# RMSNorm with ReLU on one core: two small zero writes to the output rows, queued between the prefetch loads

## Chip, cores, metric

One core of a Trainium2 chip. Times are device microseconds; a kernel's time is the median of several executions. The span is the profiled part of one execution, about 1.7 us shorter. All runs with a known state were in the fast state, with a granted clock of 1.00; a single run of a kernel has no known state, and its time is only a rough one.

## The reference

```python
# x: (16, 1024, 512) float32, gamma: 512, eps: 1e-5
rms = np.sqrt(np.mean(x ** 2, axis=-1, keepdims=True) + eps)
return np.maximum(x / rms * gamma, 0).astype(np.float32)
```

The 16384 rows of 512 floats are read once and written once: 33.55 MB each way.

## The kernel before

The rows are cut into 8 chunks of 4 MB. In a chunk every one of the 128 partitions holds 16 rows, 32 KB that lie together in HBM. There are six slots in SBUF (the core's on-chip memory), so six chunks are loaded ahead; chunk 0 comes in two halves, so that the computation starts early (ScalarE's first square at 8.78 us). All loads and stores are issued by SyncE (SP) on one queue:

```python
xv = x2.rearrange("(c p k) d -> c p k d", p=P, k=K)      # K = 16
ov = out2.rearrange("(c p k) d -> c p k d", p=P, k=K)
loads = [(0, 0, G), (0, G, K - G)] + [(i, 0, K) for i in range(1, nchunks)]   # G = 8
...
for m, (i, a, r) in enumerate(loads):
    if i < nslots:                      # nslots = 6
        load(m)
nxt = nslots
for i in range(nchunks):
    nc.sync.wait_ge(done, per * (i + 1))      # DVE has finished chunk i
    store(i)
    if i >= 1 and nxt < nchunks:
        nc.sync.wait_ge(sem_st[nxt - nslots], 16)   # the slot is stored
        ...load of chunk nxt...
        nxt += 1
```

ScalarE (ACT) squares and sums the rows and takes the root; VectorE (DVE) takes the reciprocal, multiplies by it and by gamma in place, and applies the maximum in place, in groups of 8 rows per partition.

## Time and profile before

| | before |
|---|---|
| time, median of 6 runs | 162.82 us (162.61 to 162.89) |
| profiled span | 161.2 us |
| DMA bytes | 67.1 MB, 97.4% of 16 engines' span |
| DVE busy / ACT busy | 126.0 / 86.3 us |

The page's groups of instructions (line, engine, operation, tiles, count; busy us, mean ns; idle before them) show where DVE's time goes, and its list of DMA issues (count, KB each, us from issue to landing) how long the transfers lie in the queue:

```profile
L139 DVE SCALAR_TENSOR_TENSOR slots<-slots,rstd,gamma_sb 128x512 f32 x128 | 86.2, 747 | 4.8 <-DVEq L136 4.8
L146 DVE TENSOR_SCALAR slots<-slots x16 | 36.7, 2294 | 2.4 <-DVEq L145 0.2
...
out_dram<-slots SPq DMA_DIRECT2D x8, 4096.0 KB, 31.4
slots<-in_x_dram SPq DMA_DIRECT2D x7, 4096.0 KB, 30.4
```

A 4 MB transfer takes 9.7 us on the engines but 30 us from issue to landing: by these medians some three transfers are queued at a time. DVE works steadily, but its sum is 35 us below the span.

**How the hole is measured.** The trace records every DMA packet. A row of 32 KB takes 1.213 us on its engine. "Hole" below is the extra time over 1.213 us of the last three rows before a change of direction, each row's mean over the 16 engines, summed. The expectations on record used the interval between completions instead, which reads about 0.02 to 0.05 us more.

### The profile page before, as it was taken

The page shows a single profiled execution, that of the slowest core. Times are in us where ns is not written, and L with a number is a line of the kernel's source. Part 1 is how long each engine was busy: PE and PEld are TensorE (multiplying, and loading weights), DVE is VectorE, ACT ScalarE, POOL GpSimd, SP SyncE. Part 2 cuts the span into 40 slices and gives each one's busy share as a digit, 9 for nine tenths or more (in the row PEclk, how much of TensorE's full clock was granted, in tenths as well). Part 3 has the DMA queues.
Part 4 walks back from the last instruction along what each step waited for, and adds up shares of the span by engine and source line. Part 5 has one row for each costly group of instructions (what it writes and reads, how often), then busy time and mean ns, then how long its engine had stood idle before and what let it go on. Part 6 is the DMA issues. An engine that isn't in the chain of part 4 may idle for free. (4 is left out here: it accounts for less than half of the span.)

```text
span 161.2 us, 1006 instructions
## 1 busy us (share of the span) xinstructions
DVE 126.0 (78%) x164; ACT 86.3 (54%) x273; POOL 0.2 (0%) x4
## 2 busy tenths in 40 slices
DVE  1103989898989898999999999999999999993000
ACT  3088929889988988988900298503994000000000
POOL 0000000000000000000000000000000000000000
DMA  5999999999999999999999999999999999999993
GB/s 155 433 439 431 496 390 415 496 390 399 512 390 390 512 399 390 390 399 512 390 399 504 399 399 496 407 399 488 407 407 488 407 407 480 415 407 464 431 390 138
DMA packets 2456, 67.12 MB, mean 416 GB/s; under 512 B 276, under 2 KB 276, under 8 KB 280
## 3 DMA queue, kind: packets, MB, share of 16 engines
q1 hardware_dynamic: 2448, 67.11, 97.4%
q10 hardware_dynamic: 8, 0.01, 0.0%
HBM read 33.56 MB, written 33.55 MB: 416 GB/s over the span
## 5 line engine op out<-in xcount | busy, mean ns | idle before, releaser
L115 ACT ACTIVATE junk<-slots 128x512 f32 x128 | 74.5, 582 | 30.8 <-ACTq L111 30.5
L139 DVE SCALAR_TENSOR_TENSOR slots<-slots,rstd,gamma_sb 128x512 f32 x128 | 86.2, 747 | 4.8 <-DVEq L136 4.8
L146 DVE TENSOR_SCALAR slots<-slots x16 | 36.7, 2294 | 2.4 <-DVEq L145 0.2
L115 ACT ACTIVATION_READ_ACCUMULATOR junk<-slots x128 | 23.9, 187 | 0.0
L133 DVE RECIPROCAL rstd<-rms x16 | 3.2, 197 | 6.4 <-DVEq L129 6.4
L122 ACT ACTIVATE rms<-ss,eps_sb x16 | 4.8, 301 | 3.0 <-ACTq L121 3.0
L126 DVE LOAD_MASK_SELECT gamma_sb<-gseed x1 | 0.0, 14 | 5.8 <-DMA gseed<-in_gamma_dram 5.8
L107 ACT ACT_TABLE_LOAD x1 | 1.3, 1283 | 2.8 <-issue 2.8
L100 DVE MEMSET gseed<- 128x512 f32 x1 | 0.5, 485 | 1.1 <-SPq L81 1.1
L126 DVE STREAM_SHUFFLE gamma_sb<-gseed 128x512 f32<-128x512 f32 x1 | 0.7, 716 | 0.0
L168 POOL MEMSET const-bfloat16-1.0<- 128x1 bf16 x1 | 0.1, 102 | 0.0
L168 POOL MEMSET const-uint8-127<- 128x1 uint8 x1 | 0.1, 102 | 0.0
L168 POOL MEMSET const-float32-1.0<- 128x1 f32 x1 | 0.1, 99 | 0.0
L168 POOL MEMSET const-float32-0.0<- 128x1 f32 x1 | 0.1, 98 | 0.2 <-issue 0.2
L101 DVE MEMSET eps_sb<- 128x1 f32 x1 | 0.1, 59 | 0.0
## 6 DMA issues: line engine op xcount, KB each, us to landing
out_dram<-slots SPq DMA_DIRECT2D x8, 4096.0 KB, 31.4
slots<-in_x_dram SPq DMA_DIRECT2D x7, 4096.0 KB, 30.4
slots<-in_x_dram SPq DMA_DIRECT2D x2, 2048.0 KB, 9.7
gseed<-in_gamma_dram ACTq DMA_DIRECT2D x1, 8.0 KB
```

Source lines behind the costliest of these rows:

```text
L100: nc.vector.memset(gseed, 0.0).then_inc(sem_z, 1)
L101: nc.vector.memset(eps_sb, eps).then_inc(sem_e, 1)
L107: nc.scalar.preload_act_table(ACTF.Sqrt)
L115: a = nc.scalar.activation(out=junk[:, j, :], in_=slots[:, bass.ds(base + j * d, d)], func=ACTF.Square, accum_out=ss[:, bass.ds(col + j, 1)])
L122: nc.scalar.activation(out=rms[:, bass.ds(col, G)], in_=ss[:, bass.ds(col, G)], func=ACTF.Sqrt, bias=eps_sb, scale=inv_d).then_inc(sq, 1)
L126: nc.vector.stream_shuffle(gamma_sb, gseed, [0] * 32)
L133: nc.vector.reciprocal(out=rstd[:, bass.ds(col, G)], in_=rms[:, bass.ds(col, G)]).then_inc(sv, 1)
L139: r = nc.vector.scalar_tensor_tensor(out=row, in0=row, scalar=rstd[:, bass.ds(col + j, 1)], in1=gamma_sb, op0=ALU.mult, op1=ALU.mult)
L146: nc.vector.tensor_scalar_max(out=blk, in0=blk, scalar1=0.0).then_inc(done, 1)
L168: nc = _bacc.Bacc("TRN2", target_bir_lowering=False, num_devices=1)
```

## The change

The intent: the stream loses about 0.7 us where it turns from loads to the first store. Two tiny stores to the rows that the first store will write, called touches below and queued earlier, are to take that cost at a point where it can be hidden. What they write is overwritten by the real store; the changed kernel issues that store only when they have landed (52.37 us).

```diff
+    zeros = singles.tile([P, 32], F32, name="zeros")
+    sem_w = tc.alloc_semaphore("touch")
+    sem_wz = tc.alloc_semaphore("touchz")
...
+        ntouch = 0
         for m, (i, a, r) in enumerate(loads):
             if i < nslots:
                 load(m)
+                if nslots - 3 <= i < nslots - 1 and a + r == K:
+                    if ntouch == 0:
+                        nc.sync.wait_ge(sem_wz, 1)
+                    nc.sync.dma_start(out=ov[0][:, ntouch, 0:32],
+                                      in_=zeros).then_inc(sem_w, 16)
+                    ntouch += 1
+        nc.sync.wait_ge(sem_w, 16 * ntouch)
...
+        nc.vector.memset(zeros, 0.0).then_inc(sem_wz, 1)
```

## The prediction

> **What bounds the kernel now.** I read the page first, then the stages of the span, the landings of each transfer, the waits of the queue that issues the transfers, and the timeline of the end.
>
> The page's busy table, the DMA rows of its slices and its table of queues (packets, MB, share of 16 engines):
>
> ```profile
> DVE 126.0 (78%) x164; ACT 86.3 (54%) x273; POOL 0.2 (0%) x4
> DMA  5999999999999999999999999999999999999993
> q1 hardware_dynamic: 2448, 67.11, 97.4%
> ```
>
> The DMA engines are full from the first microseconds to the end, at 97.4% of 16 engines' span; DVE is busy for 78% of it. The single queue q1 carries all loads and all stores. The packet records of the trace say how it runs: a 32 KB row takes 1.21 us on one of the 16 engines, each engine has 8 of the 128 rows of a transfer, so a 4 MB transfer takes 8 x 1.21 = 9.68 us, and in 16 of the 17 transfers (the two 2 MB ones count as half) one follows the other with no gap. 16 x 9.68 = 154.9 us of the 161.2 us span is therefore bytes. What is left, about 6.3 us, is: 1.95 us until the first packet (0.94 us to the first issue and 1.0 us from there), about 0.8 us in which the first packets are slow, about 1.2 us by which the last DMA engine ends after the first one, 1.6 us after the last data, and one hole in the middle of about 0.7 us.
>
> That hole is what the change is about. In equal stretches of the span, one transfer long (start:end, length, DVE, ACT and POOL busy, clock, DMA share, GB/s):
>
> ```profile
> 41.14:50.82 9.68, 9.23 (x14) 9.21 (x32) 0.00 (x0) 1.00 1.01 433
> 50.82:60.50 9.68, 9.23 (x13) 8.73 (x29) 0.00 (x0) 1.00 1.08 433
> 60.50:70.18 9.68, 9.09 (x13) 8.73 (x29) 0.00 (x0) 1.00 0.91 393
> 70.18:79.86 9.68, 9.23 (x11) 9.21 (x32) 0.00 (x0) 1.00 1.00 430
> 79.86:89.54 9.68, 8.94 (x13) 0.88 (x3) 0.00 (x0) 1.00 1.00 433
> ```
>
> 433 GB/s everywhere, but 393 GB/s in the stretch in which the last prefetched load ends and the first store begins. 40/433 of 9.68 us is 0.9 us, cut by the edges of the stretch; the packet records give the better size. The sixth whole load (chunk 5) has its last two rows on every engine at 1.21 to 1.66 and 1.54 to 1.96 us in place of 1.21, and the first engine's completion comes 10.36 us after that of the load before, not 9.68. So 0.68 us are lost once, at 58.5 to 61.5 us. The later changes from a load to a store and back cost nothing measurable (intervals of 9.68 us again). It is a thing of the first write to the output, or of the first read of SBUF by DMA.
>
> The issuing queue's waits (who, for whom, us in total, times, longest):
>
> ```profile
> SPq L78 <- DVE slots L146: 105.4, 6, 26.6
> SPq L74 <- DMA out_dram<-slots: 32.9, 2, 24.1
> ```
>
> and its timeline in the middle (start, length, what):
>
> ```profile
> 31.14 16.83 SPq L78 DMA_DIRECT2D out_dram<-slots  x2
> 72.07 0.34 SPq L74 DMA_DIRECT2D slots<-in_x_dram  x1
> ```
>
> The queue waits long, but early: the first store is issued at 31.1 and the second at about 48.0, while the engines reach the first store only at 61.5, behind six chunks of loads. The end of the computation against the end of the queue:
>
> ```profile
> 144.20 2.29 DVE L146 TENSOR_SCALAR slots<-slots  x1
> 146.52 0.33 SPq L78 DMA_DIRECT2D out_dram<-slots  x1
> ```
>
> DVE ends at 146.5 and the last store is issued there; the engines finish the store before it at 148.7. With 1.0 us from issue to first packet, the last store is ready about 1.1 us before it is needed. DVE is thus the next bound, close behind.
>
> [...] the store issued at 31.1 moves no byte before 61.5. [...] the 4 B semaphore writes of the trace take 9 ns each and the gamma packets of 2048 B 84 ns. [...] a packet follows a semaphore write within 6 ns.
>
> **The change part by part.**
> 1. DVE: one memset of 128x32, ahead of the one of 128x512. The 128x1 memset took 59 ns and the 128x512 one 485, so about 0.08 us. It delays gamma, which is there at 7.4 us and needed at 15.0: 0.
> 2. Issue: two more transfers at about 0.4 us each on the queue that issues loads, the first behind the fourth chunk's load. The engines have about 40 us of work queued then: 0.
> 3. The new wait before the first store ends when the second small write has landed, behind the fifth chunk. That load ends at about 51.7 us in the trace; [...] the first store is issued at about 54 in place of 31.1, the second directly after it. The engines need it at 61.5. Slack about 7 us: 0. The refill of a slot, issued when the first store has landed (72.1), does not move.
> 4. DMA work: per engine 2 x 8 packets of 128 B and two semaphore writes. If one costs what a 4 B semaphore write costs (9 ns), that is 16 x 9 = 0.15 us; if it costs a gamma packet's 84 ns, 1.3 us. I choose 30 ns: about +0.5 us, all on the path, since the engines have no gap in which to hide it.
> 5. The intended gain: the first-write stall is taken by 128 B writes, [...] and not by a stream of 32 KB writes. At best -0.68 us.
> Sum, if the stall is hidden: 162.7 - 0.7 + 0.5 = 162.5. At the very best 162.0 to 162.1.
>
> **Rivals.**
> A. The stall moves and does not vanish: the ring stops for the first small write as it stopped for the first store. For it: the stall showed in the packets of the load *ahead* of the store, so it may block whatever is in the engine, whatever the size of the write. Against it: nothing. Then 162.7 + 0.5 = 163.2, with a hole at about 42 us instead of 60.
> B. Each small write makes a hole of its own: [...] The start shows what that costs: the first row of 16 KB takes 1.2 to 1.5 us against 0.61, some 0.7 us. Twice that, with or without the stall saved: 163.4 to 164.6. Against it: semaphore descriptors between loads make no hole. [...]
> C. DVE takes over as the bound: it would eat a gain above about 1.1 us. A gain of 0.7 stays below it.
> D. The stall is not tied to writing the output, or is tied to each 4 MB area or row: the touches cover 256 B of each row of chunk 0 alone. Then the stall stays at 60 us and the touches cost 0.5: 163.2. Against the area: the stores of later chunks, to areas never touched, have no stall.
>
> **Range and chances.** Stall hidden (0.45): 162.0 to 162.8. Moved or kept (0.3): 162.9 to 163.6. Own holes (0.2): 163.4 to 164.6. Worse (0.05). The middle of this lies at about 162.7, and I predict 162.6 us, 161.9 to 164.1. Faster by 2% means under 159.5, a gain of 3.2 us, and no term reaches that: 0.01. Slower by 2% means over 165.9, [...]: 0.04. Within 2%: 0.95.
>
> **What would show it.** Right: the stretch at 60 us at about 433 GB/s, packets of 128 B at some tens of ns, no wait at the first store that ends after 61.5, the first store landed at about 71.9 or earlier. Wrong in step 5: a hole near 42 or 52 us of about 0.7, or the one at 60 still there. Wrong in step 4: two slow spots behind the fourth and fifth loads with sum over 1 us. Wrong in step 3: the first store issued after 61.5, with an idle DMA there. Wrong altogether: a last store that waits for DVE, or a time below 161.9.

## The result, and the profile after

| | before | after |
|---|---|---|
| median | 162.82 us (162.61 to 162.89, 6 runs) | 162.88 us (162.74 to 163.09, 6 runs) |
| ratio after/before | | 1.0006 (95%: 0.9993 to 1.0019) |

Ratios here are the mean time of one kernel's fast runs over that of the other's from the same rounds, so not quite the ratio of the medians. Two later comparisons of the same pair on other chips gave 1.0007 (0.9990 to 1.0024) and 1.0000 (0.9987 to 1.0013). The kernels are equal to about 0.2%.

The page after, the rows that answer to those of before (busy, DMA by slices, packets, queue), and the issues of the new transfer:

```profile
DVE 126.1 (78%) x165; ACT 86.3 (54%) x273; POOL 0.2 (0%) x4
DMA  5999999999999999999999999999999999999993
DMA packets 2744, 67.15 MB, mean 417 GB/s; under 512 B 564, under 2 KB 564, under 8 KB 568
q1 hardware_dynamic: 2736, 67.14, 97.6%
...
out_dram<-zeros SPq DMA_DIRECT2D x2, 16.0 KB, 43.4
```

There are 288 packets more: 256 of 128 B and 32 semaphore writes. The other rows of the page differ only in what follows from these, in line numbers and in small scatter. The same equal stretches of the span as for before:

```profile
41.14:50.82 9.68, 9.23 (x14) 9.21 (x32) 0.00 (x0) 1.00 1.02 435
50.82:60.50 9.68, 9.23 (x13) 8.73 (x29) 0.00 (x0) 1.00 1.06 435
60.50:70.18 9.68, 9.08 (x13) 8.73 (x29) 0.00 (x0) 1.00 0.94 406
70.18:79.86 9.68, 9.23 (x11) 9.21 (x32) 0.00 (x0) 1.00 1.00 433
```

The stretches with the touches (41 and 51 us) lose nothing visible. The stretch at 60 us is still the slow one, at 406 GB/s against 393 before: the hole is still there. By packets it is 0.39 us, against 0.72. The GB/s of a stretch only show where the hole lies; for its size they are too coarse, since the hole's place against the stretch's edges counts too. The same stretch of c1_after and of e1_wait_only, two runs told of below:

```profile
60.50:70.18 9.68, 9.08 (x13) 8.73 (x29) 0.00 (x0) 1.00 0.91 393
60.50:70.18 9.68, 9.08 (x13) 8.73 (x29) 0.00 (x0) 1.00 0.92 396
```

The first has a hole of 0.57 us by packets and the second one of 0.78, in the opposite order. So sizes below are by packets.

The issuing queue's waits (who, for whom, us in total, times, longest), and its timeline (start, length, what):

```profile
SPq L77 <- DMA out_dram<-slots: 27.2, 2, 18.8
SPq L100 <- DVE slots L160: 25.5, 1, 25.5
SPq L81 <- DMA out_dram<-zeros: 21.2, 1, 21.2
```

```profile
3.63 0.47 SPq L94 DMA_DIRECT2D out_dram<-zeros  x1
4.14 0.44 SPq L77 DMA_DIRECT2D slots<-in_x_dram  x1
4.63 0.49 SPq L94 DMA_DIRECT2D out_dram<-zeros  x1
...
52.38 0.82 SPq L81 DMA_DIRECT2D out_dram<-slots  x2
71.98 0.34 SPq L77 DMA_DIRECT2D slots<-in_x_dram  x1
```

The new wait of 21.2 us looks large in a list of waits and costs nothing: it ends at 52.4 us, and the engines reach the first store at 61.4. The refill of the first slot is issued at 71.98 us, against 72.07 before.

How small the cost of a touch is, the DMA summary of the 1.5 us around the first of them shows:

```profile
DMA packets 176, 0.54 MB, mean 361 GB/s; under 512 B 160, under 2 KB 160, under 8 KB 160
```

Its 128 data packets and their semaphores pass within the same beat: the packet records give 13 ns for a 128 B packet, one starting 9.5 ns after the other. On average over the engines, the row behind the first touch starts 1.302 us after the row ahead of it, against 1.216 at the same place before, and at the second touch 1.301 against 1.221: 0.087 and 0.080 us more. From chunk 3's first row to chunk 5's seventh, where the hole begins, the stream takes 26.83 us against 26.67: both touches cost 0.16 us. (An expectation below puts it at 0.19, which counts the load's own semaphore too.)

**Where the 0.2 us between the two profiled spans is.** Averaged over the 16 engines, the last transfer's final semaphore packet starts at 158.70 us before and 158.64 after: 0.06 us. The last engine alone is at 159.55 and 159.35. So 0.14 of the 0.20 us is by how much one DMA engine lags at the end, which differs from trace to trace (the second trace of before has 159.67, the later two of after 159.43 and 159.52). The means of those three are 158.74, 158.68 and 158.76: no order between the kernels.

### The profile page after: what moved, and what is told of

Same layout as the page of the kernel before. It is cut to its first block, busy times and chain, and to the rows that moved or that the text cites. A ratio compares the mean times of both kernels' runs of the same rounds, so it can differ in the third digit from the quotient of the medians.

```text
span 161.0 us, 1010 instructions
## 1 busy us (share of the span) xinstructions
DVE 126.1 (78%) x165; ACT 86.3 (54%) x273; POOL 0.2 (0%) x4
```

## The experiments

The theory to be tested is that of the prediction: the hole is the first write to the output (or DMA's first bulk read of SBUF), and an early small write takes part of it away. The rivals: the smaller hole came from the later issue of the first store; it is chance; the hole has another cause. Twelve runs were made, in three batches, each on one chip (called A, B, C here; batch A is c0, e1, e2, e3; batch B c1, e4, e5, e6; batch C e7, e8, e9, c2; for the first pair the chip isn't recorded). All were correct.

| run | chip | touches | hole ahead of first store, us | device time, us |
|---|---|---|---|---|
| before | | no | 0.72 | 162.82 |
| c0_before | A | no | 0.86 | 163.06 (1 run) |
| e1_wait_only | A | no, late issue | 0.78 | 163.69 (1 run) |
| e2_touch_last | A | chunk 7, early issue | 0.78 | 163.21 (1 run) |
| e3_store_early | A | no | 0.94 at 40 us | 163.08 (1 run) |
| after | | yes | 0.39 | 162.88 |
| c1_after | B | yes | 0.57 | 162.81 |
| e4_touch_last_late | B | chunk 7, late issue | 0.55 | 162.70 (1 run) |
| e6_touch8 | B | eight | 0.39 | 163.41 (1 run) |
| c2_after | C | yes | 0.57 | 162.84 |
| e5_store_row_early | B | a row of results, 256 KB | 0.45, and 0.15 ahead of the row store | 162.76 |
| e7_long_read_later | C | no | 0.00; 0.90 behind it, 0.69 ahead of the second store | 163.53 (1 run) |
| e8_sbuf_copy | C | no | 0.00; 0.73 ahead of the copy | 172.56 (1 run) |
| e9_hbm_copy | C | no | 0.30; 0.00 ahead of the copy | 174.32 (1 run) |

The kernel before, timed in the same batches, took 162.96 us on chip A (1 run), 162.78 on B (7 runs) and 162.83 on C (11 runs).

### c0_before and c1_after, c2_after: the same two kernels again

No edit.

> The kernel before, unchanged, for a second trace of it. In the first trace the interval between the completions of chunk 4's and chunk 5's loads (mean over the 16 DMA engines) was 10.42 us in place of 9.68: a hole of 0.74 us. If the hole is a fixed thing of the first store, it is 0.7 to 0.8 again. If its size is left to chance, then the smaller hole of the changed kernel (10.12 there, 0.43) may be chance too, and this run shows something else, say 0.4 or 1.0.

The stretches of c0 (same columns):

```profile
50.82:60.50 9.68, 9.23 (x13) 8.73 (x29) 0.00 (x0) 1.00 1.09 433
60.50:70.18 9.68, 9.09 (x13) 8.73 (x29) 0.00 (x0) 1.00 0.90 389
```

389 GB/s: the hole comes again, with 0.86 us by packets (0.72 before): in both traces of this kernel it stands at the same place, with a size that varies.

> The changed kernel, unchanged, for a second trace and more times. The hole ahead of the first store was 0.43 us in its first trace, against 0.74 and 0.90 in two traces of the kernel before and 0.79 to 0.96 in three experiments. If the touches do help: about 0.4 again. If that was chance: 0.7 to 1.0. Time against before: -0.1 to +0.2 us.

> The changed kernel again, for a third trace and the narrowest interval on the time. With holes of 0.39 and 0.58 us (touches' own share taken out) in its two traces against 0.74 and 0.90 in two of the kernel before, the touches would save about 0.3 and cost 0.19: -0.1 us, so a ratio of 0.999 to 1.000. If a third trace shows 0.7 or more, even the 0.3 is chance, and the ratio is 1.001.

Holes 0.57 and 0.57 us; medians 162.81 against 162.78 and 162.84 against 162.83 us of before on the same chips; the ratios are given above. The mean hole of the three traces of the changed kernel is 0.51 us, of the two of before 0.79. That looks like a gain of 0.28 for a cost of 0.16. But no trace of the kernel before was taken on chips B and C, so that difference is not cleanly separated from the chip.

### e1_wait_only: the late issue without touches

```diff
+        nc.sync.wait_ge(sem_ld[5], 16)      # chunk 4 has landed
         nxt = nslots
```

> No touches; only the first store's issue is put off to when chunk 4 has landed (52 us in place of 31), as the change does as a side effect. If the touches made the hole smaller: hole 0.74 as in the kernel before. If the late issue did: hole about 0.4. Time within 0.3 us of before in both cases.

Hole 0.78 us, against 0.72 and 0.86 in the two traces of before: no effect of the late issue alone shows. The time of 163.69 us is from another place: one DMA engine lags by 1.9 us at the end of this trace, against 1.2 before.

### e2_touch_last and e4_touch_last_late: touches to another area

```diff
-                    nc.sync.dma_start(out=ov[0][:, ntouch, 0:32],
+                    nc.sync.dma_start(out=ov[nchunks - 1][:, ntouch, 0:32],
```

In e4 that is the whole difference from the changed kernel. In e2 the wait for the touches is moved as well, to ahead of the last store, so that the first store is issued at 31 us.

> The two touches write to chunk 7's rows and the wait for them stands ahead of the last store, so the first store is issued at 31 us as before. If writing anything to the output early is what makes the hole smaller: hole about 0.4. If the touch must hit the rows of the first store (an area's first write), or if the late issue did it: 0.74.

> The changed kernel with one difference: the touches write to chunk 7's rows in place of chunk 0's. If the touch must hit the rows of the first store: hole 0.7 to 0.95. If any early write together with the late issue helps: 0.4.

e2: 0.78 us, no less than c0 and e1 on the same chip. e4: 0.55 us, as c1 on the same chip. So by these traces it does not matter which rows the touches write: whatever they do, they warm no particular area. Whether they do anything stays open: e2 says no, and on chip B there is no trace of the kernel before. One reading fits every trace and was not tested: that only touches and a late first store together shorten the hole. With both it is 0.39 to 0.57 us (after, c1, c2, e4, e6); the late issue alone (e1) and the touches alone (e2) leave 0.78. The kernel that has both was not traced on chip A.

### e6_touch8: more touches

```diff
+                    for _ in range(4):
+                        nc.sync.dma_start(out=ov[0][:, 2 * ntouch, 0:32],
+                                          in_=zeros).then_inc(sem_w, 16)
+                        ntouch += 1
```

> Eight touches of 128 B per row in place of two, at rows 0, 2 .. 14 of each partition of chunk 0. Cost 8 x 0.09 = 0.75 us of DMA time. If each touched place takes part of the hole away: hole at 60 us under 0.2. If the amount doesn't matter: 0.4 as with two; if touches do nothing: 0.8.

Hole 0.39 us against 0.57 with two on the same chip, for 0.63 us of DMA time (27.30 against 26.67 us over the stretch used above); 163.41 us in its one run, against 162.78. The six more touches cost in proportion (0.47 us) and gained less than that (0.18 us).

### e5_store_row_early: a touch that writes real results

```diff
+            if i == 4:
+                nc.sync.wait_ge(done, 1)
+                nc.sync.dma_start(out=ov[0][:, 0, :],
+                                  in_=slot_ap(0)[:, 0, :]).then_inc(sem_r, 16)
...   (the first store writes rows 1 to 15; both are waited for)
```

> A touch that costs no extra bytes: row k=0 of each partition of chunk 0 (2 KB each, 256 KB in all, real results) is stored between the loads of chunks 3 and 4, and the first store writes the other 15 rows. If early writes in the first store's area warm something: no hole or one under 0.3 at the row store at 41 us, hole at 60 us at most 0.4, and the kernel is 0.3 to 0.5 us faster than before. If a hole comes with the first writes of any large size: 0.3 to 0.7 at 41 us already, and 0 to 0.4 at 60; time as before. If writes never warm anything: 0.8 at 60.

The load ahead of the row store has 0.15 us of extra time, the one ahead of the first store still 0.45: 0.60 together, as much as c1's one hole on the same chip. The median is 162.76 us against 162.78, ratio 1.0005 (0.9988 to 1.0021). The version without extra bytes gains nothing either.

### e3_store_early: the first store ahead of two loads

```diff
+            if i == 4:
+                nc.sync.wait_ge(done, per)
+                store(0)
             if i < nslots:
                 load(m)
...   (the loop of stores then begins with chunk 1)
```

> No touches; the first store is put in the queue between the loads of chunks 3 and 4 (issued at 31 us, while chunk 3's load still runs). If the hole belongs to the first full store: it moves to about 40 us (in the load of chunk 3) and is 0.7 us there, and 60 us has none. If it belongs to the sixth load, or to that moment: it stays at 60 us. If it comes from stores that follow six loads without a break: none.

```profile
31.46:41.14 9.68, 9.22 (x13) 8.73 (x29) 0.00 (x0) 1.00 1.10 433
41.14:50.82 9.68, 9.23 (x13) 9.21 (x32) 0.00 (x0) 1.00 0.89 383
50.82:60.50 9.68, 9.23 (x13) 6.24 (x21) 0.00 (x0) 1.00 1.00 433
60.50:70.18 9.68, 9.09 (x13) 6.79 (x22) 0.00 (x0) 1.00 1.00 433
```

The slow stretch has moved with the store from 60 to 41 us (0.94 us by packets) and 60 us is clean. Here the hole goes with the change from loads to a store, not with a moment or the sixth load. Ahead of the second store, after two loads, there are 0.15 us.

### e8_sbuf_copy: a bulk read of SBUF that writes no HBM

```diff
+        nc.sync.wait_ge(done, per)
+        nc.sync.dma_start(out=slot_ap(5), in_=slot_ap(0)).then_inc(sem_r, 16)
         load(5)                              # chunk 4
+        nc.sync.wait_ge(sem_r, 16)
         load(6)                              # chunk 5
```

> One transfer of 4 MB more, from SBUF to SBUF, behind chunk 3's load (41 us; chunk 5's load then overwrites what it wrote). It costs about 9.7 us and is not meant to be fast. If the hole is the first time that DMA reads SBUF in bulk: the hole of 0.7 to 1.0 stands ahead of the copy at 41 us and the first store at about 71 us has none. If it is the first bulk write to HBM: none at 41, 0.7 to 1.0 ahead of the first store.

```profile
31.46:41.14 9.68, 9.00 (x12) 8.73 (x29) 0.00 (x0) 1.00 1.08 433
41.14:50.82 9.68, 9.23 (x13) 9.21 (x30) 0.00 (x0) 1.00 0.91 393
50.82:60.50 9.68, 9.23 (x14) 6.47 (x22) 0.00 (x0) 1.00 1.00 433
60.50:70.18 9.68, 9.11 (x12) 6.80 (x22) 0.00 (x0) 1.00 1.00 433
70.18:79.86 9.68, 9.21 (x11) 9.02 (x30) 0.00 (x0) 1.00 1.00 430
```

393 GB/s and 0.73 us at the copy, although it stays inside SBUF; and no hole (0.00 us by packets) ahead of the first store at 71 us, the first transfer that writes to the output. So a hole of this size needs no write to HBM, and the first write to the output need not have one. **The hole is not the first write to HBM**, which is what the touches were meant for. (The first store here stands behind two loads only, as e3's second store did, which lost 0.15 us; the short run may be a part of its zero.)

### e9_hbm_copy: a bulk write of HBM that reads no SBUF

```diff
+        nc.sync.dma_start(out=ov[nchunks - 1], in_=xv[nchunks - 1]).then_inc(sem_r, 16)
         load(5)
```

> One transfer of 4 MB more, from the input straight to chunk 7's part of the output (wrong data, overwritten by the last store), behind chunk 3's load. Costs 9.7 us or more. If the hole is the first bulk write to HBM: 0.7 to 1.0 at 41 us, none ahead of the first store. If it is the first bulk read of SBUF: none at 41, 0.7 to 1.0 ahead of the first store at about 71 us. If it is a first write into each area: at both.

```profile
41.14:50.82 9.68, 9.23 (x14) 9.21 (x32) 0.00 (x0) 1.00 1.16 433
50.82:60.50 9.68, 9.23 (x13) 6.25 (x21) 0.00 (x0) 1.00 0.84 325
60.50:70.18 9.68, 9.09 (x13) 5.32 (x17) 0.00 (x0) 1.00 1.00 433
```

There is no hole ahead of the copy (0.00 us by packets). The copy itself takes 11.3 us in place of 9.7, and the load behind it 10.5; that is the slow stretch. Ahead of the first store at 73 us, after two loads, 0.30 us are left. This agrees with e8 that writing HBM does not bring the hole on, but more weakly: within the 1.6 and 0.8 us that the copy and the load behind it take too long, a stall could hide. It doesn't fit a plain "first read of SBUF" well, which asked for 0.7 to 1.0.

### e7_long_read_later: is it the first change, or a change after many loads?

```diff
-   loads of chunks 0 to 5, then the stores, each slot refilled when stored
+   loads 0 1 2, store 0, loads 3 4 5 6, store 1, store 2, load 7, stores 3 ...
```

> No touches. Queue order: loads of chunks 0 to 2, first store, loads of chunks 3, 4, 5, 6, second store. If the hole is a thing of the first store: 0.7 to 1.0 us in chunk 2's load ahead of the first store (about 31 us), and at most 0.15 ahead of the second store (about 80 us), although four loads run before it without a break. If it comes from a long run of loads being turned round: the large hole stands ahead of the second store, and the one ahead of the first is no larger.

```profile
31.46:41.14 9.68, 9.17 (x13) 8.73 (x29) 0.00 (x0) 1.00 1.09 433
41.14:50.82 9.68, 9.23 (x14) 4.86 (x17) 0.00 (x0) 1.00 0.90 379
...
79.86:89.54 9.68, 8.94 (x13) 8.73 (x29) 0.00 (x0) 1.00 1.03 423
```

Neither expectation held whole. Ahead of the first store (32 us) there is no stretched row; that store was issued at 31.1 us, when the last load queued ahead of it had only 0.8 us left. Whether that is why there is no stretched row isn't shown. A hole of 0.90 us stands instead at the end of that store, where the queue turns back to loads: the store's last row takes 0.72 us too long and the next load's first 0.17. And a second large hole, 0.69 us, stands ahead of the second store, after four loads in a row. So a large hole can come twice in one execution, and it is not the first store's alone.

## Why the prediction was right or wrong

The time of 162.88 us lies in the range of 161.9 to 164.1 and "within 2%" was right, for the reason given: no term of the sum is as large as 2%. By its steps:

1. **The memset** took 85 ns, as estimated (0.08 us), and delayed nothing.
2. **The issues** took 0.47 and 0.49 us (estimated 0.4), in front of a full queue: no cost, right.
3. **The wait** ended at 52.4 us, expected at about 54, which was the author's estimate. The second touch landed 0.17 us after the load ahead of it (52.37 against 52.19 us). Slack 9 us instead of 7: no cost, right.
4. **The cost of the small writes** was mis-sized: 0.16 us, not 0.5. A 128 B packet takes 9.5 ns of the stream (13.5 GB/s on its engine, against 27 for a 32 KB row), not the 30 ns chosen between a semaphore write (9 ns) and a gamma packet (84 ns). The lower bound given, 9 ns each or 0.15 us, was nearly the truth.
5. **The gain** is the step that failed: "the first-write stall is taken by 128 B writes". That small writes would take it was the author's assumption; no trace had shown it. At best 0.68 us was given, and 0.33 was seen in the first pair of traces, 0.28 between the means. The touches pass without a stall, as the step supposed, but they don't take the store's: no row at 42 or 51 us is stretched by more than 0.011 us, and more than half of the hole stays at 60 us. The premise behind it, "the first write to the output", falls with e8, where the hole stands at a copy that writes no HBM. The other half of that sentence, "the first read of SBUF by DMA", can't be the whole cause either: in e7 a hole of 0.69 us stands at the second store, and in e9 the first bulk read of SBUF lost 0.30 us.

The sum came out as 162.5 by too high a cost and too high a gain, by 0.3 and by 0.4 us, so the two errors nearly cancel; that the number is this close is luck. It also started from 162.7 where 162.82 was measured. With the measured terms it is 162.82 - 0.28 + 0.16 = 162.70 us; the 0.18 us to the measured 162.88 is within the interval of the ratio (0.0013 of 162.8 is 0.21). The middle was drawn wrongly from the prediction's own chances, too: 0.45 lies below 162.8 and 0.55 above 162.9, so it is at 162.8 to 162.9, not at 162.7.

Of the rivals, A (the stall moves to the touch) and B (each touch makes a hole of its own) are excluded by the rows next to the touches, 1.213 to 1.224 us each. C did not come into play: DVE ended at 146.5 us in both. D, that the stall is not tied to writing the output, is what the runs support, and its other half, an area or row that must be touched, is not: the rows touched don't matter (e4 against c1). D's cost of 0.5 was too high, as in step 4.

**What stays open.** The runs show where the hole stands, not its cause. The large ones, 0.39 to 0.94 us, stood at the first turn of the full queue from loads to a bulk transfer out of SBUF (all kernels but e5, e7 and e9), at e7's first turn back to loads, and at its turn after four loads. Turns after two loads, with one bulk transfer already done, lost 0.00 (e8), 0.15 (e3), 0.30 (e9) and, after e5's small store, 0.45 us. Later turns after single loads cost 0.02 us at most in the kernel before, and up to 0.14 (e3). That is a trend with the length of the run of loads, or with the time since DMA last read SBUF in bulk. The two went together except in e9, where SBUF had not been read in bulk at all and two loads lost only 0.30 us; that speaks for the length of the run, but it is one trace, with a copy ahead of the loads. Within four to six chunks there is no trend: four lost 0.69 to 0.94 us (e7, e8, e3), six 0.72 to 0.86. Whether small touches shorten the hole at all is open too, since e2 saw nothing and the comparisons that saw something crossed chips. No version was found that beats both kernels, and none is claimed: the nearest, e5, is equal.

## What to carry to other kernels

Before paying for a warm-up, find out what the cold thing is: one experiment with the other half of the transfer (e8, SBUF to SBUF) showed a hole of 0.73 us with no write to HBM, and so ruled the first write out as the cause. With the queue full from end to end (97.4% of 16 engines' span), a whole hole of 0.7 us was worth 0.4% at most, so read a change of that size from packet times of several traces on one chip; two single traces (0.72 and 0.39 us) suggested an effect that the clock never showed. The wait of 21.2 us on the issuing engine cost nothing here: it ended at 52.4 us, and the engines had queued loads to work on until 61.4 us.
